# Turning all attention weights by VectorE squares and copies within SBUF, on one core of Trainium2

## The chip, the cores and the metric

One core of a Trainium2 chip runs the kernel. Its engines each work through a queue of their own: TensorE (PE; its weight loads are shown apart as PEld), VectorE (DVE), ScalarE (ACT), GpSimd (POOL), and SyncE (SP), which issues the transfers (DMA). Tiles lie in SBUF (128 partitions) or in PSUM, the accumulators of TensorE. The metric is the device time of one execution in microseconds; before the change it is the median of three runs, 765.46 us (765.05 to 765.88).

## The reference

One encoder layer, for a prompt of 1024 frames and a sample group of 32 frames with a past of 512, in float32, width 1024:

```python
u = rmsnorm(h, g_pre) @ w_in                 # qA kA vA gA qB kB vB gB
# A: 8 heads of 64, a frame sees its 64-frame chunk and the 8 chunks before it
s = einsum('bqhd,bkhd->bhqk', q, k) * ATTN_SCALE + bias_table[:, rel]
oA = einsum('bhqk,bkhd->bqhd', softmax(where(ok, s, NEG_INF)), v)
# B: 8 heads of 64, stick-breaking, causal = (k_pos < q_pos)
z = einsum('bqhd,bkhd->bhqk', q, k) * ATTN_SCALE
log_1m = where(causal, log_sigmoid(-z), 0.0)
after = cumsum(log_1m, axis=3, reverse=True) - log_1m
oB = einsum('bhqk,bkhd->bqhd', where(causal, exp(log_sigmoid(z) + after), 0.0), v)
y = concat(oA * silu(gA), oB * silu(gB)) @ w_out
h = h + rmsnorm(y, g_post)
h = h + sigmoid(h @ w_ple_gate) * (p @ w_ple)
```

The new keys and values are outputs as well.

## The kernel before

**Stages.** The frames are normalised and turned; the projection is made in 32 pieces (8 kinds times 4 pairs of heads, over 3 chunks of 352 frames; PSUM tiles `mm_kB3_2` and the like: kind kB, pair 3, chunk 2); the 16 heads of attention are woven into it, the heads of a kind and pair as soon as their q, k and v are there; the output projection and the gate (`oB`, `gB`, `sum_dro`, `sggA`) end the kernel. Every float32 product is made from a high and a low half (names with h and l, such as `hnh` and `hnl`, `wTh` and `wTl`), in three matmuls.

**A head.** `attention(ab, p, h)` works for kind A or B, pair p, head h; A30 is kind A, pair 3, head 0. It goes over 8 blocks of 128 queries. Block i of B meets i + 1 blocks of keys, block i of A at most 5 (128 to 640 columns). `scores(i)` makes the scores in PSUM tiles of tag S (two pieces, where there are over 512 columns). For A, VectorE adds the bias and takes the minimum (`om`, `stat`), and ScalarE's Exp writes `be`. For B, VectorE adds a mask to the diagonal 128 columns, ScalarE's Sigmoid writes `om`, VectorE's scan multiplies along the row from the right, and GpSimd's subtraction of neighbours writes `be`. `weights_t(i)` turns the weights so that keys lie on partitions, and splits them in the halves `wTh` (a cast on ScalarE) and `wTl` (a subtraction on VectorE). `values(g)` makes the product with v for four blocks of queries (`PV`, g = 0 or 1), first with `wTh`, then with `wTl`; ScalarE and VectorE add the two halves of the result up into `ot` (`otA30_0` is g = 0).

**Two ways to turn.** `ROUND` (line 32) names the blocks that are turned without TensorE: blocks 4 to 7 of A, 4 to 6 of B, one at a time. There VectorE transposes squares of 32 x 32 (STREAM_TRANSPOSE `om<-be`), one transfer writes the result to DRAM in another order (`swapA<-om`), another brings it back (`be<-swapA`), and the halves are made from SBUF. All other blocks are turned by TensorE (`ptw`, up to four 128 x 128 squares in one PSUM tile of tag T), and the halves are made from PSUM. The sample's attention (`sample_attention`: SsA, SsB, QsA, ptks, ptws) uses the same PSUM tags.

**What sets the order.** A `Recorder` collects all operations with what each depends on. `plan()` then sets one order for all engines by a table of costs (`cost()`), `due()` gives due times for 42 further passes, and `settle()` applies some 230 moves by hand (`MOVES`, line 44). `emit()` (line 552 in the profile, whose rows all bear it) issues the operations in that order. Each engine's queue is worked off strictly in order. PSUM has 8 banks: `PS_BUFS = {"mm": 2, "S": 3, "T": 2, "PV": 1}`.

Of the kernel before, what the change touches and what calls it, by code (L numbers as in the profile page):

```python
# [14 lines left out]
P = 128  # L15
# [16 lines left out]
ROUND = {"A": ((4,),(5,),(6,),(7,)), "B": ((4,),(5,),(6,))}  # L32
# [11 lines left out]
MOVES = (  # L44
# [28 lines left out]
)  # L73
PASSES, SPREAD = 42, 400
# [134 lines left out]
class Op:  # L209
    __slots__ = ("eng", "what", "args", "kw", "key", "busy", "late", "ready", "left", "after", "at", "size", "shared", "table")  # L210


LAND = {"PE": 165, "ACT": 0, "DVE": 0, "POOL": 0, "SP": 0, "CTL": 0}
SEM = 60
WAKE = {"PE": 400, "ACT": 100, "DVE": 100, "POOL": 190, "SP": 0}
ISSUE, ISSUE_64, ISSUE_SHORT = 470, 610, 660
DMA_RATE, LANDING, WAKE_DMA = 320.0, 2500, 200
TABLE_NS = 1310
DVE_SET, POOL_SET = 137, 110
# [79 lines left out]
class Recorder:  # L299
# [35 lines left out]
    def node(self, eng, what, args, kw, after):  # L335
        o = Op()
        o.eng, o.what, o.args, o.kw, o.after = eng, what, args, kw, after
        o.key = (self.cls if eng == "PE" else self.low, len(self.ops))
        o.shared, o.table, o.busy, o.late = False, None, 0.0, 0.0
        self.ops.append(o)  # L340
        return o

    def add(self, eng, what, args, kw):
# [22 lines left out]
        o.busy, o.late = self.cost(eng, method, args, kw, writes, reads)  # L366
        o.shared = eng == "POOL"
        o.table = next((a for a in args if a in (AF.Exp, AF.Sigmoid)), None) if eng == "ACT" else None
        if eng == "DVE":
            sbuf = [v for v in reads if isinstance(v, (View, Segments)) and not v.buf.psum and v.free() > 4]  # L370
            o.shared = len(sbuf) > 1 or (method == "tensor_copy" and len(sbuf) == 1 and not writes[0].buf.psum)

    @staticmethod
    def cost(eng, method, args, kw, writes, reads):

# [9 lines left out]
        if eng == "DVE":  # L385
            if method == "tensor_tensor_scan":
                return 150 + 2.1 * n, 85
# [1600 lines left out]
```

## Time and profile before

| | |
|---|---|
| median of three runs | 765.46 us |
| span of the profiled execution | 764.2 us |
| granted clock of TensorE | 1.000 |
| HBM read and written | 107.62 MB and 65.30 MB |
| transfers on SP's queue | 736 |
| VectorE instructions on the weights' way in the order: STREAM_TRANSPOSE `om<-be` / wTl from SBUF / wTl from PSUM | 56 / 56 / 80 |

The profile is of one execution. Each group is written as line, engine, operation, output<-input (partitions x elements), then the count, the busy time in microseconds and the mean of one in nanoseconds, then the idle time of the engine just ahead of these instructions and what ended it. In a timeline a row has its start, its length, the engine and the operation; neighbours of one kind are joined with their count.

### The profile page before, as it was taken

Reading aid. Unit: us, or ns where it says so; the run is one execution under the profiler, and the core shown is the slowest. Engines: PE = TensorE matmul, PEld = TensorE weight load, DVE = VectorE, ACT = ScalarE, POOL = GpSimd, SP = SyncE. Lnnn points to the kernel's source line nnn. Section 1 sums busy time; section 2 is a strip of 40 time slices with the busy share of each in tenths; the row PEclk is TensorE's granted clock in tenths of the full one; section 3 lists DMA queues with packets and bytes.
Section 4 is the critical chain, followed back from the end, with each engine's and each line's share of the span. In section 5 each row is a group of like instructions: output and inputs, shape, how many; then the busy total and the mean of one; then the engine's idle time right before and its main releaser. Section 6 shows DMA issues by size and latency. Waiting matters only on the chain.

```text
span 764.2 us, 13673 instructions
## 1 busy us (share of the span) xinstructions
PE 757.5 (99%) x4422; PEld 702.8 (92%) x4422; DVE 582.2 (76%) x1025; ACT 490.2 (64%) x995; POOL 455.2 (60%) x525
## 2 busy tenths in 40 slices
PE   9999999999999999999999999999999999999997
PEld 7999999999999999999999999999998877888786
DVE  6826789888899888988998798884554588587665
ACT  5736686567685658785668685633447868774551
POOL 5705637874344546566882346786543769898443
PEclk9999999999999999999999999999999999999999
DMA  8519998877976649999678789787688859879854
GB/s 275 175 36 277 294 297 280 236 235 252 247 225 187 181 135 283 275 317 293 173 243 274 173 244 275 222 255 225 192 271 267 275 161 330 278 250 336 277 183 139
DMA packets 184826, 182.25 MB, mean 238 GB/s; under 512 B 42177, under 2 KB 139497, under 8 KB 184754
## 3 DMA queue, kind: packets, MB, share of 16 engines
q1 hardware_dynamic: 184754, 181.37, 78.3%
q8 instruction: 35, 0.57, 0.3%
q14 instruction: 37, 0.30, 0.1%
HBM read 107.62 MB, written 65.30 MB: 226 GB/s over the span
## 4 chain that ended last, share of the span: by engine, by line
PE 99%; DMA 1%; DVE 0%; SPq 0%; issue 0%
PE mm_qA L552 6%; PE mm_kA L552 6%; PE mm_vB L552 6%; PE mm_vA L552 6%; PE mm_gA L552 6%; PE mm_gB L552 6%; PE mm_kB L552 6%; PE mm_qB L552 6%; PE SB L552 5%; PE PVB L552 4%; PE PVA L552 4%; PE SA L552 4%; PE ple L552 3%; PE g1P L552 3%; PE o3P L552 3%; PE o1P L552 3%
## 5 line engine op out<-in xcount | busy, mean ns | idle before, releaser
L552 POOL TENSOR_TENSOR be<-om 128x128 f32<-128x128 f32 (+7 forms) x64 | 77.9, 1224 | 57.1 <-DVE om L552 29.8
L552 DVE TENSOR_TENSOR_SCAN om<-om,SB 128x384 f32<-128x384 f32 (+5 forms) x96 | 94.5, 998 | 7.6 <-ACT om L552 5.0
L552 DVE TENSOR_TENSOR wTl<-be,wTh 128x640 fp32r<-128x640 f32 (+2 forms) x56 | 60.7, 1087 | 5.3 <-ACT wTh L552 5.2
L552 ACT ACTIVATE om<-SB 128x384 f32<-128x384 f32 (+5 forms) x96 | 45.0, 492 | 29.3 <-PE SB L552 12.4
L552 ACT ACTIVATE be<-om,statA 128x640 f32<-128x640 f32 (+3 forms) x64 | 46.4, 730 | 14.6 <-DVE wTl L552 7.3
L552 DVE STREAM_TRANSPOSE om<-be 128x640 f32<-128x640 f32 (+2 forms) x56 | 49.6, 891 | 5.4 <-ACT be L552 3.4
L552 ACT CAST wTh<-be 128x640 fp32r<-128x640 f32 (+2 forms) x56 | 43.1, 776 | 12.3 <-DMA be<-swapA 6.6
L552 ACT CAST wTh<-ptwB 128x512 fp32r<-128x512 f32 (+3 forms) x48 | 22.1, 485 | 20.5 <-PE ptwB L552 15.1
L552 DVE CUSTOM_DVE_ANT_0 om<-SA,biasA 128x320 f32<-128x320 f32 (+3 forms) x64 | 29.7, 483 | 6.9 <-PE SA L552 6.2
L552 POOL TENSOR_TENSOR gB<-gB,gB 128x256 f32<-128x256 f32 x32 | 25.9, 828 | 12.3 <-DMA gB<-in_w_ple_gate_dram 6.2
L552 PE MATMUL SB<-klB,LB 128*128 128x384 f32 (+5 forms) x96 | 33.0, 347 | 0.0
L552 PE MATMUL SB<-kdB,LB 128*128 128x384 f32 (+5 forms) x96 | 32.5, 344 | 0.0
L552 DVE TENSOR_TENSOR wTl<-ptwB,wTh 128x512 fp32r<-128x512 f32 (+3 forms) x48 | 25.3, 541 | 6.6 <-PE PVB L552 3.9
L552 POOL TENSOR_TENSOR oB<-oB,oB 128x256 f32<-128x256 f32 x32 | 26.1, 841 | 6.8 <-DMA oB<-in_w_out_dram 6.7
L552 PE MATMUL SA<-klA,LA 128*128 128x320 f32 (+2 forms) x96 | 29.5, 319 | 0.0
L552 PE MATMUL SA<-kdA,LA 128*128 128x320 f32 (+2 forms) x96 | 29.4, 316 | 0.0
L552 DVE TENSOR_TENSOR SB<-SB,maskb 128x128 f32<-128x128 f32 x64 | 18.3, 291 | 14.3 <-PE SB L552 13.8
L552 POOL TENSOR_TENSOR sggA<-sggA,oggA 128x352 f32<-128x352 f32 x24 | 25.6, 1069 | 5.7 <-DMA o_dr<-otA 2.7
L552 POOL TENSOR_TENSOR klB<-stkB,kdB 64x1024 fp32r<-64x1024 f32 x8 | 19.2, 2396 | 10.7 <-ACT kdB L552 7.3
L552 POOL TENSOR_TENSOR klA<-stkA,kdA 64x1024 fp32r<-64x1024 f32 x8 | 19.5, 2436 | 8.1 <-ACT kdA L552 7.8
L552 POOL TENSOR_TENSOR h<-h,x 128x512 f32<-128x512 f32 (+1 forms) x18 | 23.1, 1295 | 1.5 <-DVE h L552 1.4
L552 POOL TENSOR_TENSOR sggB<-sggB,oggB 128x352 f32<-128x352 f32 x12 | 13.2, 1100 | 14.4 <-DVE sggB L552 14.4
(683 smaller groups left out, 2591.1 us busy)
## 6 DMA issues: line engine op xcount, KB each, us to landing
swapA<-om SPq DMA_DIRECT2D x32, 320.0 KB
be<-swapA SPq DMA_DIRECT2D x32, 320.0 KB
oB<-in_w_out_dram SPq DMA_DIRECT2D x16, 256.0 KB
sum_dro<-oB SPq DMA_DIRECT2D x16, 256.0 KB
gB<-in_w_ple_gate_dram SPq DMA_DIRECT2D x16, 256.0 KB
sum_drg<-gB SPq DMA_DIRECT2D x16, 256.0 KB
x<-in_x_prompt_dram SPq DMA_DIRECT2D x16, 256.0 KB
turned<-hs SPq DMA_DIRECT2D x16, 256.0 KB
```

What stands on the lines that cost most here:

```text
L552: getattr(getattr(tc.nc, o.what[0]), o.what[1])(*args, **kw)
```

## The change

`ROUND` becomes `((0,1,2,3),(4,),(5,),(6,),(7,))` for both kinds. Blocks 0 to 3 of a head are turned together, with 1280 columns; block 7 of B, with 1024, is turned like the others. No weight of the prompt is turned by TensorE (224 transposes go). A round's two transfers through DRAM become four copies within SBUF, each from 32 source partitions to all 128. The operation ahead (Exp of A, the subtraction of B) writes `be` in the order that one transpose of the whole round needs. Neighbouring blocks of a round are split into halves by one cast and one subtraction. The mask of B goes from VectorE, ahead of the sigmoid, to GpSimd, behind it, as a fill with 1.0. PSUM tag S has four buffers and T one. `plan()`, `cost()`, `due()`, `settle()`, `MOVES` and their constants go: `ORDER` holds, for each engine, the numbers of its operations in the order in which they are issued.

```diff
-ROUND = {"A": ((4,),(5,),(6,),(7,)), "B": ((4,),(5,),(6,))}
+ROUND = {"A": ((0, 1, 2, 3), (4,), (5,), (6,), (7,)), "B": ((0, 1, 2, 3), (4,), (5,), (6,), (7,))}
...
-MOVES = (
-    (4286, 4279), (4263, 4256), (2107, 2084), (9133, 9126), (3839, 3830), (1137, 1124), (110, 105), (5252, 5215), (100, 94), (682, 676), (1066, 1059),
...
+ORDER = {
+    "PE": """
+0-23 48-53 24-27 54-61 28-31 62-71 84-85 32-35 72-81 36-39 86 82-83 87-89 40-43 90-95 120-123 144 44-47 145-147 124-132 96-99 133-143 148-149 100-103 150-160
...
-    PS_BUFS = {"mm": 2, "S": 3, "T": 2, "PV": 1}
+    PS_BUFS = {"mm": 2, "S": 4, "T": 1, "PV": 1}
...
+        def first(i):
+            g = together[i]
+            return sum(cost(x) for x in g[:g.index(i)])
+
-        def apart(i, x, out=False):
+        def apart(i):
 
             if i not in together:
-                return x
-            return x.rearrange("p (c k d) -> p k c d" if out else "p (k c d) -> p k c d", c=2, d=2)
+                return rooms(i)[1]
+            g = together[i]
+            n = sum(cost(x) for x in g) * P
+            rooms(i)
+            return whole[g][1][:, 0:n].rearrange("p (c k d) -> p k c d", c=2, d=2)[:, first(i) * 32:(first(i) + cost(i)) * 32]
+
+        def keys(i, x):
+            return x.rearrange("p (k c d) -> p k c d", c=2, d=2) if i in together else x
...
-                dg = s[:, b - a - P:b - a]
-                nc.vector.tensor_tensor(dg, dg, maskb, ALU.add)
                 nc.gpsimd.memset(w0[:, n:n + 1], 1.0)
                 for a, b, s in pieces:
                     nc.scalar.activation(w0[:, a:b], s, AF.Sigmoid, scale=-1.0)
+                nc.gpsimd.affine_select(out=w0[:, n - P:n], in_=w0[:, n - P:n], pattern=[[-1, P]], base=0, channel_multiplier=1, compare_op=ALU.is_gt, fill=1.0)
...
-                nc.gpsimd.tensor_tensor(apart(i, w1[:, 0:n], True), apart(i, w0[:, 1:n + 1]), apart(i, w0[:, 0:n]), ALU.subtract)
+                nc.gpsimd.tensor_tensor(apart(i), keys(i, w0[:, 1:n + 1]), keys(i, w0[:, 0:n]), ALU.subtract)
...
-                for x, _, _ in done_with:
-                    y = slice(first[x], first[x] + cost(x))
-                    nc.vector.transpose(squares[:, :, :, y], w1[:, y.start * P:y.stop * P].rearrange("p (i b k j) -> p i j b k", i=2, k=32, j=2))
-                dr = scratch([4, P, m * 32], f"swap{nm}_{i}")
-                dma(dr.rearrange("g (k c) x -> (g k) (c x)", c=4), w0[:, 0:m * P])
-                dma(w1.rearrange("p (g x) -> p g x", g=4), dr.rearrange("g p x -> p g x"))
-                turned = w1.rearrange("p (g b q) -> p g b q", g=4, q=32)
-                for x, hi, lo in done_with:
-                    src = turned[:, :, first[x]:first[x] + cost(x), :]
-                    hi, lo = (y.rearrange("p (b g q) -> p g b q", g=4, q=32) for y in (hi, lo))
+                nc.vector.transpose(squares, w1[:, 0:m * P].rearrange("p (i b k j) -> p i j b k", i=2, k=32, j=2))
+                for g4 in (0, 2, 1, 3):
+                    dma(w1[:, g4 * m * 32:(g4 + 1) * m * 32], w0[32 * g4:32 * g4 + 32, 0:m * P].rearrange("k (c x) -> k c x", c=4))
+                turned = w1[:, 0:m * P].rearrange("p (g b q) -> p g b q", g=4, q=32)
+                runs = []
+                for x, c in sorted(done_with):
+                    if runs and runs[-1][1] + runs[-1][2] * P == c and runs[-1][0] + runs[-1][2] == first(x):
+                        runs[-1][2] += cost(x)
+                    else:
+                        runs.append([first(x), c, cost(x)])
+                for x, c, k in runs:
+                    src = turned[:, :, x:x + k, :]
+                    hi, lo = (y[:, c:c + k * P].rearrange("p (b g q) -> p g b q", g=4, q=32) for y in wT[g])
                     nc.scalar.copy(hi, src)
                     nc.vector.tensor_tensor(lo, src, f(hi), ALU.subtract)
```

The written order differs from the planned one over the whole of the attention. Two places are shown; in the rows, the line (552 before, 493 of the changed kernel) is followed by the operation, output<-input with their numbers, and the columns.

First place, TensorE before, from the end of PVA30_0 (head A30, blocks 0 to 3) towards the sample's scores SsA1:

```order
L552 MATMUL PVA30_0_5246<-wTl_188,v2A30_4836 128x128
L552 MATMUL ptksA11_5290<-ident_179,be_211 128x128 x4
L552 MATMUL mm_kB3_2_5148<-hnh2_175,wl_kB3_0_4814 128x352
L552 MATMUL SA31_1_0_5306<-kdA31_4990,LA31_4995 128x256
L552 MATMUL SA31_1_0_5306<-klA31_4994,LA31_4995 128x256
L552 MATMUL mm_kB3_2_5148<-hnh2_175,wl_kB3_0_4814 128x352 x2
L552 MATMUL mm_kB3_2_5148<-hnh2_175,wl_kB3_1_4861 128x352 x4
L552 MATMUL mm_kB3_2_5148<-hnl2_178,wh_kB3_0_4878 128x352
```

Behind these rows stand 30 more projection matmuls of kB3 and qB3 ahead of the first SsA1, and more between the SsA1. TensorE at the same place after the change:

```order
L493 MATMUL PVA30_0_5252<-wTl_131,v2A30_4901 128x128
L493 MATMUL mm_qB3_2_5191<-hnl2_122,wh_qB3_1_4980 128x352
L493 MATMUL SA31_2_0_5379<-kdA31_4939,LA31_4941 128x384
L493 MATMUL SA31_2_0_5379<-klA31_4940,LA31_4941 128x384
L493 MATMUL SsA1_0_5317<-Kh0sA1_4741,QsA1_5377 128x272
L493 MATMUL SsA1_272_5329<-Kh0sA1_4741,QsA1_5377 128x272
L493 MATMUL SsA1_0_5317<-Kl0sA1_4754,QsA1_5377 128x272
L493 MATMUL SsA1_272_5329<-Kl0sA1_4754,QsA1_5377 128x272
```

One projection matmul now stands between PVA30_0 and SsA1. Behind the twelve SsA1 follow SA31_4_1 to SA31_6_1, four matmuls of mm_vB3_0 and PVA30_1. VectorE at this place before and after, from the addition otA30_0 on (ISA is the bias and minimum of A's scores; the small rows fill `stat`):

```order
L552 TENSOR_TENSOR otA30_0_5003<-PVA30_0_5246,otA30_0_5003 64x512
L552 ISA om_197,statA31_1_5200<-SA31_1_0_5306,biasA31_5220 128x256
L552 ISA statA31_1_5200 128x1
L552 STREAM_TRANSPOSE om_197<-be_211 128x640
L552 RECIPROCAL sumsA30_4084<-sumsA30_4084 128x8
L552 TENSOR_TENSOR Kl1sA1_5138<-ptksA11_5290,Kh1sA1_5115 128x512
L552 TENSOR_TENSOR wTl_188<-be_211,wTh_527 128x4x5x32
L552 STREAM_TRANSPOSE ktB3_5235<-stkB3_5039 128x1056
```

```order
L493 TENSOR_TENSOR otA30_0_5188<-PVA30_0_5252,otA30_0_5188 64x512
L493 ISA om_138,statA31_0_5267<-SA31_0_0_5273,biasA31_5272 128x128
L493 ISA statA31_0_5267 128x1
L493 ISA om_138,statA31_1_5318<-SA31_1_0_5331,biasA31_5272 128x256
L493 ISA statA31_1_5318 128x1
L493 STREAM_TRANSPOSE om_138<-be_145 128x640
L493 ISA om_138,statA31_2_5330<-SA31_2_0_5379,biasA31_5272 128x384
L493 ISA statA31_2_5330 128x1
L493 STREAM_TRANSPOSE om_138<-be_145 128x640
L493 TENSOR_TENSOR wTl_131<-be_145,wTh_476 128x4x5x32
L493 RECIPROCAL sumsA30_4225<-sumsA30_4225 128x8
L493 TENSOR_TENSOR LB30_5277<-stqB3_5143,LB30_5277 64x1024
```

After the change two transposes of 640 columns stand behind otA30_0. Behind LB30 follow QsA1, a second subtraction of 5 blocks, the two SsA1, SA31_3_0 to SA31_4_1 with a third subtraction, the transpose of 1280 columns, and the fourth subtraction.

Second place, TensorE after the change, from the end of PVB10_0 (head B10) to the sample's scores SsB0:

```order
L493 MATMUL PVB10_0_3079<-wTl_131,v2B10_2685 128x128
L493 MATMUL mm_qA2_2_3249<-hnh2_119,wh_qA2_1_2897 128x352 x4
L493 MATMUL mm_qA2_2_3249<-hnh2_119,wl_qA2_0_2882 128x352 x4
L493 MATMUL mm_qA2_2_3249<-hnh2_119,wl_qA2_1_2898 128x352 x4
L493 MATMUL mm_qA2_2_3249<-hnl2_122,wh_qA2_0_2881 128x352 x2
L493 MATMUL SB11_2_0_3307<-kdB11_2682,LB11_2684 128x384
L493 MATMUL SB11_2_0_3307<-klB11_2683,LB11_2684 128x384
L493 MATMUL mm_qA2_2_3249<-hnl2_122,wh_qA2_0_2881 128x352 x2
L493 MATMUL mm_qA2_2_3249<-hnl2_122,wh_qA2_1_2897 128x352 x4
L493 MATMUL SsB0_0_3182<-Kh0sB0_2991,QsB0_3300 128x272
```

There the twelve SsB0 follow, with PVB10_1 among them. VectorE there, from otB10_0 on, before and after (SCALAR_TENSOR_TENSOR is the scan):

```order
L552 TENSOR_TENSOR otB10_0_3110<-PVB10_0_3184,otB10_0_3110 64x512
L552 TENSOR_TENSOR Kl1sB0_3031<-ptksB01_3160,Kh1sB0_3012 128x512
L552 TENSOR_TENSOR SB11_1_0_3268<-SB11_1_0_3268,maskb_181 128x128
L552 STREAM_TRANSPOSE ktA2_3099<-stkA2_2807 128x544
L552 TENSOR_TENSOR Kl0sB0_2977<-ksS_184,Kh0sB0_2955 128x32
L552 SCALAR_TENSOR_TENSOR om_197<-om_197,SB11_1_0_3268 128x256
```

```order
L493 TENSOR_TENSOR otB10_0_3080<-PVB10_0_3079,otB10_0_3080 64x512
L493 TENSOR_TENSOR wTl_131<-be_145,wTh_476 128x4x5x32
L493 SCALAR_TENSOR_TENSOR om_138<-om_138,SB11_0_0_3128 128x128
L493 TENSOR_TENSOR wTl_131<-be_145,wTh_476 128x4x6x32
L493 SCALAR_TENSOR_TENSOR om_138<-om_138,SB11_1_0_3216 128x256
L493 TENSOR_TENSOR wTl_131<-be_145,wTh_476 128x4x7x32
L493 TENSOR_TENSOR QsB0_3300<-QfsB0_3092,QsB0_3300 128x256
L493 TENSOR_TENSOR LA20_3133<-stqA2_2807,LA20_3133 64x1024
L493 TENSOR_TENSOR wTl_131<-be_145,wTh_476 128x4x8x32
```

All four subtractions of the second half (5 to 8 blocks of keys) now stand behind otB10_0, and behind the last of them the scans of SB11_2_0 and of the sample.

More of the change, by code (lines that the diff above doesn't have):

```diff
@@ L1 @@
-import random
 from contextlib import ExitStack
@@ new lines @@
+3151-3166 3232-3235 3167-3170 3236-3239 3171-3174 3177-3194 3240-3383 3388-4197
+""",
+    "ACT": """
+0 4 2 1 3 5 7-8 6 15-17 9 18 10 19-20 12 11 22 25 13-14 28 21 23 33 24 38 26 34 27 41 30 29 37 31-32 44 39 47 40 42 48 43 45-46 49 35 50 36 53 61 51 62 55 52 60
+63-65 54 67-68 74 56 66 73 80 71 77 70 69 57 79 58 81 76 75 86 78 83 59 72 82 84 88 90 105 89 91 85 92 98 101 93 99 97 96 87 94-95 106 104 107 100 108 111 103
+118 102 109 121 110 112 123 122 125-126 113 119 114 120 128 124 129 127 133 132 136 131 135 115 139 116 142 144 150 138 143 148 141 137 130 134 117 147 140
@@ new lines @@
+758 754 765 764 753 771 770 760 774 768 776-777 775 766 783 779 781 767 784 780 785 761 794 786-787 778 795 798 797 772-773 799 796 788-789 782 803 800 807-808
+805-806 812 811 790-793 815 804 818 809 801-802 820 814 813 810 824 816 822 817 826 819 825 829 821 830 827 833-834 831 823 836 828 835 838 832 837 840 839 842
+841 843-846 848 847 849 851 850 852-856 858 857 859-860
+""",
+    "POOL": """
+0 4 1 48 65 2-3 9-10 5-6 11 7-8 12-13 15-16 14 19 17 21 20 18 22 27-28 23 29 24 30-31 25 32 26 35-41 46-47 63-64 33-34 43 42 49-50 45 44 61 59-60 62 77 154 75
@@ L209 @@
 class Op:
[L210 to L219, printed above, removed]
+    __slots__ = ("eng", "what", "args", "kw", "after")
 class Pool:
@@ L365, in add @@
                 b.uses.append((o, v.box, write))
[L366 to L371, printed above, removed]
@@ L416, in order @@
             place.after.update(x[0] for x in old.uses)
-        users = {id(o): [] for o in self.ops}
-        for o in self.ops:
-            for a in o.after:
-                users[id(a)].append(o)
-        spread = random.Random(22)
-        best, end = self.plan(users)
-        for _ in range(PASSES):
-            self.due(best, users, end)
-            for o in self.ops:
-                if o.eng not in ("CTL", "PE"):
-                    o.key = (o.key[0] + spread.gauss(0, SPREAD), o.key[1])
-            best, end = self.plan(users)
@@ L429, in order @@
-        return self.settle(best)
-    @staticmethod
-    def settle(ops):
-        for i, j in MOVES:
-            x = ops[i]
-            need, engines, ahead, behind = set(x.after), {x.eng}, [], []
-            for o in reversed(ops[j:i]):
-                if o in need or (o.eng in engines and o.eng != x.eng):
-                    assert o.eng != x.eng
-                    ahead.append(o)
-                    need |= o.after
-                    if o.eng != "CTL":
-                        engines.add(o.eng)
-                else:
-                    behind.append(o)
-            ops[j:i + 1] = ahead[::-1] + [x] + behind[::-1]
-        return ops
@@ L449, in due @@
-    def due(self, out, users, end):
-        late, after = {}, {}
-        for o in reversed(out):
-            e = o.eng
-            t = after.get(e, end) if 0 and e != "CTL" else end
-            for u in users[id(o)]:
-                v = late[id(u)]
-                if u.eng == e and e not in ("SP", "CTL"):
-                    v -= 0.0 if e == "PE" else o.late
-                elif u.eng != "CTL":
-                    v -= SEM + WAKE[u.eng] + (WAKE_DMA if e == "SP" and u.eng != "SP" else 0) + o.late * (e != "SP")
-                elif e != "SP":
-                    v -= o.late
-                if e == "SP":
-                    v -= LANDING + o.late
-                t = min(t, v)
-            if e == "PE":
-                right = min(t, after.get(e, end)) - o.busy
-                after[e] = right
-                late[id(o)] = o.at + 1.0 * max(0.0, right - o.at)
-                continue
-            late[id(o)] = t - o.busy if e != "CTL" else t
-            if e != "CTL":
-                after[e] = late[id(o)]
-                o.key = (late[id(o)], o.key[1])
@@ new lines, in order @@
+        mine = {e: [o for o in self.ops if o.eng == e] for e in ORDER}
+        lines = {}
+        for e, text in ORDER.items():
+            runs = [[int(x) for x in run.split("-")] for run in text.split()]
+            lines[e] = [mine[e][i] for r in runs for i in range(r[0], r[-1] + 1)]
+            assert len(lines[e]) == len(set(lines[e])) == len(mine[e])
+        out, done, places = [], set(), [o for o in self.ops if o.eng == "CTL"]
+        at = dict.fromkeys(lines, 0)
+        while len(out) < len(self.ops):
+            n = len(out)
+            for o in [x for x in places if x.after <= done]:
+                out.append(o)
+                done.add(o)
+                places.remove(o)
+            for e, line in lines.items():
+                while at[e] < len(line) and line[at[e]].after <= done:
+                    out.append(line[at[e]])
+                    done.add(line[at[e]])
+                    at[e] += 1
+            assert len(out) > n
@@ L542, in emit @@
+        return out
     def emit(self, tc):
```

226 lines of the change are left out of this document (119 added, 107 removed), and 27 rows, old and new, of the table MOVES.

## The prediction
> **What bounds the kernel now.** I read three views, from coarse to fine: the page's busy times and its chain, then a window table of the attention stage.
>
> ```profile
> span 764.2 us, 13673 instructions
> PE 757.5 (99%) x4422; PEld 702.8 (92%) x4422; DVE 582.2 (76%) x1025; ACT 490.2 (64%) x995; POOL 455.2 (60%) x525
> PE 99%; DMA 1%; DVE 0%; SPq 0%; issue 0%
> 100.00:500.00 400.00, 400.00 (x2546) 388.85 (x2545) 349.23 (x621) 276.24 (x566) 232.40 (x282) 1.00 0.82 240
> ```
>
> The second line is busy time by engine, the third the chain that ended last, and the fourth the stretch from 100 to 500 us: its length, then busy time and count of PE, PEld, VectorE, ScalarE and GpSimd, then the granted clock, the DMA share and GB/s. TensorE is never idle, and its clock is 1.00. So only less TensorE work, or a gap torn into it, can move the time. The last line holds the warning: VectorE is already busy 349.23 of those 400 us (87%).
>
> **Taken from TensorE.** The transposes of the attention weights go: 144 of B and 80 of A.
>
> ```profile
> L552 PE MATMUL ptwB<-ident,be 128*128 128x128 f32 x144 | 21.6, 273 | 0.0
> L552 PE MATMUL ptwA<-ident,be 128*128 128x128 f32 x80 | 13.5, 272 | 0.0
> 409.02 0.93 PE L552 MATMUL ptwA<-ident,be 128*128 128x128 f32 x7
> 409.71 1.05 PE L552 MATMUL mm_kB<-hnl,wh_kB 128*128 128x352 f32 x5
> 70.40 0.49 PE L552 MATMUL ptwA<-ident,be 128*128 128x128 f32 x3
> 70.64 0.40 PE L552 MATMUL SA<-klA,LA 128*128 128x320 f32 x1
> ```
>
> The mean of 272 ns is pipeline depth and not what a transpose occupies. The last four rows (start, length, what) give that: seven transposes from 409.02 to 409.71 are 0.099 us each, three from 70.40 to 70.64 are 0.080 each. 224 of them are 17.9 to 22.1 us. I take 0.087, **-19.4 us**, as more of them stand in short groups like the second.
>
> **Added to VectorE.** 16 transposes of 1280 columns and 8 of 1024 come in, 64 mask additions go, and of the subtractions that make the low half (wTl) 80 from PSUM give way to 56 from SBUF: 16 each of 128, 256 and 896 columns, 8 of 1024.
>
> ```profile
> L552 DVE STREAM_TRANSPOSE om<-be 128x640 f32<-128x640 f32 x40 | 33.0, 834 | 4.3 <-ACT be L552 3.4 <-POOL be L552 0.6
> L552 DVE STREAM_TRANSPOSE vxB<-stvB 128x1024 f32<-128x1024 f32 x4 | 4.9, 1234 | 0.0
> L552 DVE TENSOR_TENSOR wTl<-be,wTh 128x640 fp32r<-128x640 f32 x40 | 40.3, 1012 | 2.6 <-ACT wTh L552 2.4
> L552 DVE TENSOR_TENSOR wTl<-be,wTh 128x896 fp32r<-128x896 f32 x8 | 9.9, 1241 | 1.1 <-ACT wTh L552 1.1
> L552 DVE TENSOR_TENSOR wTl<-ptwB,wTh 128x512 fp32r<-128x512 f32 (+3 forms) x48 | 25.3, 541 | 6.6 <-PE PVB L552 3.9 <-ACT wTh L552 2.5
> L552 DVE TENSOR_TENSOR wTl<-ptwA,wTh 128x128 fp32r<-128x128 f32 (+3 forms) x32 | 15.0, 475 | 2.8 <-PE PVA L552 1.6 <-ACT wTh L552 1.1
> L552 DVE TENSOR_TENSOR SB<-SB,maskb 128x128 f32<-128x128 f32 x64 | 18.3, 291 | 14.3 <-PE SB L552 13.8
> ```
>
> A transpose grows by 400 ns for 384 columns, so 1280 columns are about 1.50 us; the 24 are 16 x 1.50 + 8 x 1.23 = 33.9. The mask gives back 18.3. The subtractions: 229 ns for 256 columns puts 128, 256 and 1024 at 0.55, 0.67 and 1.36, so 16 x (0.55 + 0.67 + 1.24) + 8 x 1.36 = 50.2 against 25.3 + 15.0 = 40.3, +9.9. Together 33.9 - 18.3 + 9.9 = **+25.5 us**. If a small subtraction costs in SBUF what the shorter ones cost in PSUM (0.3 less), the 32 small ones make it +16. I take +20, as 128 and 256 columns have no row in SBUF. Spread over the 485 us or so of attention, 349 becomes some 366 us in a stage that TensorE would cover in 400 - 16 = 384: 95% instead of 87%. On average it still fits. What decides is whether the written order makes the two meet.
>
> **Where they don't meet: two places.** The order (shown in the section on the change) fixes on VectorE what stands between the addition that ends a head's first half (otA30_0, otB10_0) and the last wTl that its second half needs. That addition waits for the first half's last matmul, so TensorE gets only what the order puts behind that.
>
> ```profile
> 413.07 0.80 PE L552 MATMUL PVA<-wTl,v2A 128*128 128x512 f32 x4
> 413.90 0.58 ACT L552 COPY otA<-PVA 64x512 f32<-64x512 f32 x1 [0.60 <-PE PVA L552]
> 414.52 0.68 DVE L552 TENSOR_TENSOR otA<-PVA,otA 64x512 f32<-64x512 f32 x1
> 415.13 0.41 DVE L552 CUSTOM_DVE_ANT_0 om<-SA,biasA 128x256 f32<-128x256 f32 x1
> 416.92 1.46 PE L552 MATMUL mm_qB<-hnh,wh_qB 128*128 128x352 f32 x8
> 418.21 1.46 PE L552 MATMUL mm_qB<-hnh,wl_qB 128*128 128x352 f32 x8
> 420.64 0.41 PE L552 MATMUL SsA<-Kh0sA,QsA 128*128 128x272 f32 x2
> 420.88 0.41 PE L552 MATMUL SsA<-Kl0sA,QsA 128*128 128x272 f32 x2
> L552 DVE CUSTOM_DVE_ANT_0 om<-SA,biasA,statA 128x320 f32<-128x320 f32 x32 | 17.1, 539 | 2.0 <-PE SA L552 1.6
> L552 DVE CUSTOM_DVE_ANT_0 om<-SA,biasA 128x128 f32<-128x128 f32 x8 | 2.2, 278 | 1.9 <-PE SA L552 1.6 <-POOL biasA L552 0.3
> L552 DVE CUSTOM_DVE_ANT_0 om<-SA,biasA 128x512 f32<-128x512 f32 x8 | 5.5, 686 | 1.2 <-PE SA L552 1.2
> L552 DVE TENSOR_TENSOR LB<-stqB,LB 64x1024 fp32r<-64x1024 f32 x8 | 10.8, 1350 | 0.5 <-ACT LB L552 0.2
> L552 DVE TENSOR_TENSOR LA<-stqA,LA 64x1024 fp32r<-64x1024 f32 x8 | 12.7, 1589 | 5.5 <-ACT LA L552 5.3
> L552 DVE TENSOR_TENSOR_SCAN om<-om,SB 128x384 f32<-128x384 f32 x24 | 23.9, 995 | 2.0 <-ACT om L552 1.9
> L552 DVE TENSOR_TENSOR QsB<-QfsB,QsB 128x256 fp32r<-128x256 f32 x2 | 1.2, 579 | 0.0
> L552 DVE CUSTOM_DVE_ANT_0 om<-SsA,biassA 128x272 f32<-128x272 f32 x2 | 0.9, 442 | 3.2 <-PE SsA L552 3.2
> ```
>
> First place, head A30 to A31, with the sample's attention between. TensorE: a projection matmul of 352 columns starts every 0.161 us (418.21 - 416.92 over 8), one of 272 every 0.12. Behind PVA30_0 stand one projection, two scores of 384, twelve SsA, twelve scores of 320, two of 512, then projections and the high half of PVA30_1: by columns 6.4 us to the first wTl of PVA30_1. VectorE in the same stretch: one ot addition 0.61, eight scores together 3.4 (128, 256, 384 and 512 columns on a line from 0.28 to 0.69, four of 320 at 0.5), two transposes of 640 at 0.77, one of 1280 at 1.43, four subtractions at 0.94, LB 1.3, QsA 0.5 (as QsB), two SsA 0.8, small ones 0.25: 13.7 us with 0.07 off each duration, the overlap that the third row and the fourth show (414.52 + 0.68 against 415.13), and 0.65 from the matmul's end to the addition (413.87 to 414.52). 13.7 + 0.65 - 6.4 = **8.0 us** of gap. Before, some seventy projection matmuls stood there, 11 us of cover.
>
> Second place, B10 to B11: VectorE from otB10_0 to the scans of the sample has 10.7 us (four subtractions of 640 to 1024 columns 4.6, five scans of 128 to 384 together 3.3, LA20 1.5, QsB 0.5, ot and the sample's mask 0.8, with the same overlap), and 0.65; TensorE has 6.0 us of projections, SsB0 and PVB10_1. Gap **5.4 us**. With the shortest durations of subtraction and LB or LA in the trace, the two gaps are 7.0 and 4.1.
>
> **Other edits.**
>
> ```profile
> L552 POOL TENSOR_SCALAR_AFFINE_SELECT maskb<-maskb x1: 292/292/292, 1.7 to 1.7; 128x128 f32<-128x128 f32 x1
> L552 SPq DMA_DIRECT2D swapA<-om x32: 319/390/1623, 75.6 to 449.4; - x32
> L552 SPq DMA_DIRECT2D be<-swapA x32: 359/492/2756, 84.3 to 453.2; - x32
> L552 SPq DMA_DIRECT2D kdA<-kdA x8: 482/510/638, 57.3 to 390.6; - x8
> DVE wTl L552 <- ACT wTh L552: 5.2, 9, 1.1
> DVE om L552 <- ACT om L552: 5.0, 7, 1.8
> ```
>
> The mask on GpSimd: 64 x 0.292 = 18.7 us, where 232.40 of 400 are busy; hidden, but each fill stands between a sigmoid and its scan, so it adds a step for VectorE to wait. The permuted subtraction has no row: from no change to twice its 77.9 us, still under GpSimd's free time; I take no change, as the same 128 columns move. ScalarE has 24 casts fewer and stays hidden (276 of 400 busy). One PSUM buffer for sample transposes instead of two, four for scores instead of three: only a few groups use the first, so between -2 and +3, taken as 0. On the queue of SP, 320 copies replace 112 transfers: from 112 x 0.44 = 49 to 320 x 0.50 = 160 us, which moves every other issue behind them later. The trip itself has one hop less, but four issues (2.0 us) stand where two (0.88) stood. Bounds: -10 (earlier arrival, nothing waits) to +18 (1.1 us in the last round of 16 heads). The nearest row is a copy within SBUF, kdA, whose issue alone costs 0.51, so the issue decides; here taken as hidden, and kept as a rival.
>
> Last, the rest of VectorE's waits. In 100 to 500 us it waited 24 us for engines other than TensorE (the two largest are the last two rows above, 10.2 together). With 95% load that slack is no longer free. Between 0 and 24; I take a third, **+8**.
>
> **Sum.** 764.2 - 19.4 + 8.0 + 5.4 + 8 = 766.2 us of span. The median of the runs, 765.46, lies 1.26 above the profiled span, so **767.5 us**: no gain, within a fraction of a per cent. 0.2% is 1.5 us, about what a measurement of this kernel can tell from no change.
>
> **Rivals.** *TensorE stays the bound.* Waits hide, the two gaps take their short values: 764.2 - 19.4 + 7.0 + 4.1 + 1.3 = **757**. For it: TensorE idles nowhere now, and a third of the loss needs no mechanism that I can point to. Against it: the two gaps are forced by the order, and nothing gives them back.
>
> *The copies bind.* The round that turns a head's last block now needs a transpose, four issues and a landing before its PV. Where the order leaves less than about 5 us there, TensorE waits: four issues against two is 1.1 us, 16 heads make 17, and 767.5 + 16 = **783**. It decides from the point at which SP reaches a round's copies after VectorE has turned it. For it: SP's issues grow by 110 us in the attention stage. Against it: SP waits for VectorE (45.5 us for om), so it is mostly ready.
>
> ```profile
> SPq L552 <- DVE om L552: 45.5, 30, 9.8
> ```
>
> That row is SP's own waiting. [...] No row of this profile shows a source of 32 partitions.
>
> *The change doesn't do what it says* is excluded by the counts of the order: no ptw transpose is left.
>
> **How the numbers follow.** Forecast case 47% (763 to 773: the last term between 4 and 13), TensorE bound 33%, copies 20%. The range 753 to 784 reaches into both rivals: 753 is the 757 with its gaps a third shorter (11.1 / 3 = 3.7), 784 the copies case. The forecast case alone splits 3 to 14 to 30 (its middle lies 0.27% above 765.46). Faster 33 + 3 = 36%, same 14%, slower 30 + 20 = 50%.
>
> **What would show it.** The two gaps: TensorE idle before PVA30_1's wTl matmuls and before SsA1 and SsB0, 8 and 5.4 us, put down to VectorE. TensorE's busy time down by 19.4 and its idle time up by over 15. VectorE's stage at 95%. If TensorE's idle time is put down to ScalarE's wTh with copies (be from om) behind it, the second rival is right; if it is under 8 us in all, the first. I would be wrong in the whole if VectorE's shares change price: a subtraction of 1280 columns that runs against GpSimd may cost more than its line.

## The result, and the profile after

The changed kernel takes 821.3 us (median of 4 runs, 819.91 to 822.88) against 765.67 us of the kernel before beside it (4 runs, 765.05 to 766.55): a ratio of 1.0723, 95% interval 1.0700 to 1.0746. It is 7.2% slower. The forecast was 767.5 us, with 784 as the upper end.

The page of the changed kernel (span, busy times, the chain that ended last) and the window from 100 to 500 us, with columns as in the prediction:

```profile
span 818.4 us, 13597 instructions
PE 758.4 (93%) x4198; PEld 685.4 (84%) x4198; DVE 602.8 (74%) x961; ACT 491.5 (60%) x973; POOL 488.2 (60%) x589
PE 45%; DMA 17%; SPq 11%; DVE 11%; ACT 7%; issue 5%; POOL 4%; DVEq 0%; POOLq 0%; ACTq 0%
100.00:500.00 400.00, 361.31 (x2130) 337.27 (x2129) 329.31 (x521) 253.77 (x499) 232.51 (x307) 0.98 0.78 206
```

TensorE was on the chain for 99% before; now for 45%, with transfers and SP's queue together at 28%. TensorE is idle 38.7 of the 400 us, and over the whole span 60.0 us (818.4 - 758.4), where it was 6.7 before. VectorE has not become the bound: it is busy 329 us there (82%), since it waits as well. That alone speaks against the forecast, which had VectorE at 95%.

What TensorE waits for, the four largest rows of its waits (total in us, times, longest):

```profile
PE SA L493 <- DVE statA L493: 8.6, 9, 3.4
PE SsA L493 <- ACT QsA L493: 8.0, 1, 8.0
PE SsB L493 <- ACT QsB L493: 6.5, 2, 3.3
PE PVB L493 <- ACT wTh L493: 3.8, 4, 1.7
```

These rows do not end at a cause, since the engines that they name wait themselves. So the next step is the waits of ScalarE, VectorE and GpSimd, and the issues on SP's queue (duration of one: min, median, max in ns, then first and last start):

```profile
ACT wTh L493 <- DMA be<-om: 45.8, 32, 4.7
DVE om L493 <- DMA be<-om: 19.0, 10, 7.7
POOL om L493 <- DMA be<-om: 27.5, 17, 3.8
L493 SPq DMA_DIRECT2D be<-om x320: 542/602/2028, 75.8 to 594.6; - x160
```

All three wait for the copies from `om` to `be`: ScalarE for the turned weights, VectorE and GpSimd because they may not write the next scores into a piece of the `om` ring that a copy has yet to read. One issue takes SP 0.60 us at the median, so a round's four are 2.4 us and all 320 are 193 us.

### The profile page after: what moved, and what is told of

Its sections match the earlier page's. It is cut to its first block, busy times and chain, and to the rows that moved or that the text cites. A ratio compares the mean times of both kernels' runs of the same rounds, so it can differ in the third digit from the quotient of the medians.

```text
span 818.4 us, 13597 instructions
## 1 busy us (share of the span) xinstructions
PE 758.4 (93%) x4198; PEld 685.4 (84%) x4198; DVE 602.8 (74%) x961; ACT 491.5 (60%) x973; POOL 488.2 (60%) x589
## 2 busy tenths in 40 slices
DMA packets 193275, 177.01 MB, mean 216 GB/s; under 512 B 45505, under 2 KB 155113, under 8 KB 193202
## 4 chain that ended last, share of the span: by engine, by line
PE 45%; DMA 17%; SPq 11%; DVE 11%; ACT 7%; issue 5%; POOL 4%; DVEq 0%; POOLq 0%; ACTq 0%
SPq L493 11%; DMA be<-om 8%; PE mm_gB L493 6%; DVE om L493 5%; DVE wTl L493 3%; PE g1P L493 2%; PE o3P L493 2%; PE o1P L493 2%; PE g2P L493 2%; PE g0P L493 2%; PE o0P L493 2%; PE o2P L493 2%; PE g3P L493 2%; PE ple L493 2%; PE mm_vA L493 2%
## 5 line engine op out<-in xcount | busy, mean ns | idle before, releaser
L493 DVE TENSOR_TENSOR wTl<-be,wTh 128x640 fp32r<-128x640 f32 (+5 forms) x112 | 101.2, 925 | 18.3 <-ACT wTh L493 17.8
L493 ACT CAST wTh<-be 128x640 fp32r<-128x640 f32 (+5 forms) x112 | 74.7, 695 | 48.7 <-DMA be<-om 45.8
L493 DVE STREAM_TRANSPOSE om<-be 128x640 f32<-128x640 f32 (+4 forms) x80 | 83.2, 1044 | 8.9 <-POOL be L493 5.1
L493 POOL TENSOR_SCALAR_AFFINE_SELECT om<-om 128x128 f32<-128x128 f32 x64 | 33.2, 526 | 29.1 <-ACT om L493 24.2
L493 ACT ACTIVATE om<-SB 128x384 f32<-128x384 f32 (+5 forms) x96 | 43.1, 494 | 11.3 <-PE SB L493 7.3
L493 DVE CUSTOM_DVE_ANT_0 om<-SA,biasA 128x320 f32<-128x320 f32 (+4 forms) x64 | 29.2, 481 | 25.2 <-DMA be<-om 19.0
L493 PE MATMUL SA<-kdA,LA 128*128 128x320 f32 (+4 forms) x96 | 31.5, 345 | 9.6 <-DVE statA L493 8.6
L493 PEld LDWEIGHTS SA<-kdA,LA 128*128 128x128 f32 x96 | 18.8, 199 | 13.6 <-DVE statA L493 11.5
L493 PE MATMUL SA<-klA,LA 128*128 128x320 f32 (+4 forms) x96 | 29.6, 331 | 0.5 <-DMA klA<-klA 0.5
L493 POOL TENSOR_TENSOR wl_vB<-wr_vB,wh_vB 128x512 fp32r<-128x512 f32 x8 | 10.9, 1367 | 28.9 <-ACT wh_vB L493 13.4
L493 POOL TENSOR_TENSOR klB<-stkB,kdB 64x1024 fp32r<-64x1024 f32 x8 | 19.5, 2432 | 13.6 <-ACT kdB L493 13.4
L493 PE MATMUL PVB<-wTh,v2B 128*128 128x512 f32 (+1 forms) x96 | 22.2, 351 | 4.6 <-ACT wTh L493 3.8
L493 PEld LDWEIGHTS SB<-kdB,LB 128*128 128x128 f32 x96 | 18.1, 189 | 8.3 <-DVE om L493 4.2
```

What stands on the lines that cost most here:

```text
L493: getattr(getattr(tc.nc, o.what[0]), o.what[1])(*args, **kw)
```

## The experiments

Most of these kernels leave work out or put it elsewhere, so that one part of the cost can be seen by itself. The theories: **A**, the way of the copies (their issues on SP's queue, their landing, their bytes) is what the engines wait for. **B**, the written order is too tight on VectorE and ScalarE, whatever the copies cost (the forecast's own reason). Each kernel had one timed run; beside them the kernel before took 765.7 to 767.7 us, so differences under 3 us say nothing.

**One copy of four.** In `weights_t`, only the copy with g4 = 0 is issued; three quarters of the weights are not turned. Operations marked `skip` are not issued.

```diff
+                if o.skip:
+                    continue
...
                 for g4 in (0, 2, 1, 3):
                     dma(w1[:, g4 * m * 32:(g4 + 1) * m * 32], w0[32 * g4:32 * g4 + 32, 0:m * P].rearrange("k (c x) -> k c x", c=4))
+                    rec.ops[-1].skip = g4 != 0
```

> The changed kernel with one of a round's four copies issued (the first quarter of be; the other three quarters of the weights are left out, so the output differs). 80 issues on SP's queue in place of 320, a quarter of the bytes, the order of everything else as written. Theory A (the route: issues and landing of the copies are what the engines wait for): 770 to 785 us, ScalarE's wait of wTh for be from om falls from 45.8 us to under 15. Theory B (the written order itself is too tight on VectorE and ScalarE, whatever the copies cost): over 800 us. By theory A the wait of 8.0 us ahead of SsA1 shrinks too, by B it stays.

Measured: 770.88 us, 50.4 less than the changed kernel with the same order on every engine. The page's second line, ScalarE's wait for the copies, and TensorE's at the first place:

```profile
PE 746.0 (97%) x4198; PEld 681.0 (89%) x4198; DVE 601.0 (78%) x961; ACT 489.8 (64%) x973; POOL 492.9 (64%) x589
ACT wTh L496 <- DMA be<-om: 2.1, 2, 1.7
PE SsA L496 <- ACT QsA L496: 5.0, 1, 5.0
```

VectorE's load is the same to within 2 us (601.0 and 602.8), and 50 us are gone: theory A. But 5.0 of the 8.0 us ahead of SsA1 stay, so a part of that place does not hang on the other three copies.

**Small copies.** All four issued, each of a quarter of its columns; three quarters of the weights are not turned.

```diff
-dma(w1[:, g4 * m * 32:(g4 + 1) * m * 32], w0[32 * g4:32 * g4 + 32, 0:m * P].rearrange("k (c x) -> k c x", c=4))
+dma(w1[:, g4 * m * 32:g4 * m * 32 + m * 8], w0[32 * g4:32 * g4 + 32, 0:m * P].rearrange("k (c x) -> k c x", c=4)[:, :, 0:m * 8])
```

> The changed kernel with all four copies of a round issued, each of a quarter of its columns (three quarters of the turned weights are left out, so the output differs). Same bytes as with one copy, but 320 issues. If the issues on SP's queue are the price: 805 to 820 us, as the changed kernel. If the bytes and the ports are: 770 to 785 us, as with one copy. Theory B: over 800 us in both.

Measured: 802.84 us. With the bytes of one copy but all the issues, 32.0 of the 50.4 us are back; the remaining three quarters of the bytes bring 18.5. It fits neither expectation alone: issues and bytes both count, the issues more; of ports no run shows anything. The 32.0 us are not the queue's time alone, though: a round waits for four landings again, and the transfers have as many packets (the pieces in which they move) as in the changed kernel, 193275, where one copy has 158710.

**One copy and dummies.** The other three issues of a round go from a constant (`ident`) to DRAM, and nobody waits for them; three quarters of the weights are not turned.

```diff
+                    if g4 == 0:
                         dma(w1[:, g4 * m * 32:(g4 + 1) * m * 32], w0[32 * g4:32 * g4 + 32, 0:m * P].rearrange("k (c x) -> k c x", c=4))
+                    else:
+                        dma(scratch([P, 32], f"dummy{nm}_{i}_{g4}").rearrange("(k c) x -> k c x", c=4), ident[32 * g4:32 * g4 + 32, :].rearrange("k (c x) -> k c x", c=4))
```

> As one_copy (770.9 us; three quarters of the weights are left out), but the three missing copies of a round are replaced by copies of 16 KB from a constant to DRAM, for whose landing nothing waits. SP's queue has 320 issues again. If the time in SP's queue is what the issues cost (everything behind them starts later): 795 to 805 us, as small_copies (802.8). If it is that a round is complete only with its fourth copy: within 6 us of 770.9.

Measured: 790.28 us, between the two. 19.4 us come with the issues, though nobody waits for their landing: the time on SP's queue, and 3.9 MB more of writing to DRAM (240 issues of 16 KB), which this run does not separate. The other 12.6 up to small_copies appear when a round also has to wait for its fourth copy; small_copies has 23043 packets more as well, and their share was not measured. ScalarE's wait for the copies follows, 2.1, then 13.0 here, then 27.7 with the small copies:

```profile
ACT wTh L493 <- DMA be<-om: 13.0, 10, 4.1
```

**Same bytes, all partitions.** The four copies take pieces of the same size from all 128 partitions; the weights land in a wrong layout, so the turning is left out.

```diff
-dma(w1[:, g4 * m * 32:(g4 + 1) * m * 32], w0[32 * g4:32 * g4 + 32, 0:m * P].rearrange("k (c x) -> k c x", c=4))
+dma(w1[:, g4 * m * 32:(g4 + 1) * m * 32], w0[:, g4 * m * 32:(g4 + 1) * m * 32])
```

> The changed kernel with the four copies of a round taking the same bytes in as many pieces straight from all 128 partitions, in place of 32 partitions each (the weights land in a wrong layout, so the turning is left out in effect). If reading from 32 partitions is what makes the 18.5 us between small_copies and the changed kernel: 803 to 810 us. If it is the bytes alone: 816 to 824 us.

Measured: 810.22 us. 11.1 of the 18.5 us that go with the bytes are gone when the copies read from all 128 partitions; 7.4 stay. This lies on the edge of the first expectation, and the split is good to about 3 us.

**Two queues.** Two of a round's four copies are issued by ScalarE; they stand in its order by the times at which they and ScalarE's operations started in the changed kernel's profile (those lines are left out here).

```diff
+                    if g4 in (1, 3):
+                        o = rec.ops[-1]
+                        o.moved, o.what = True, ("scalar", "dma_start")
```

> The changed kernel with the last two copies of each round issued by ScalarE's queue, at the place in ScalarE's order that the profile of the changed kernel has at that time; SP keeps 160 of the 320. If SP's queue is the bottleneck: 780 to 800 us, less what 160 issues cost ScalarE. If the bytes and the landing are, or if the issues cost any engine the same: 810 us or more.

Measured: 811.24 us, 10 less than the changed kernel. The issues by queue:

```profile
L502 ACTq DMA_DIRECT2D be<-om x160: 550/572/2225, 76.5 to 585.6; - x160
L502 SPq DMA_DIRECT2D be<-om x160: 542/597/1958, 78.0 to 584.5; - x160
```

The issue costs ScalarE the same 0.57 us. Relief for SP is real, but ScalarE pays 160 x 0.57 = 91 us of its own time, which stands ahead of its casts. Expected was 780 to 800, or 810 and more: it is the second.

**Outputs first.** On SP's queue, each transfer of a finished `ot` to DRAM is put where its `ot` was ready, ahead of the copies.

```diff
+            added = rec.ops[-1]
             dma(o_dr[sidx(ab, p)][r, 4 * g * P:4 * (g + 1) * P], ot[r])
+            rec.ops[-1].ot = added
...
+        when = {id(o): t for t, o in zip(DVE_AT, lines["DVE"])}
+        both = [(min(t, when[id(o.ot)] + 72) if o.ot else t, 0 if o.ot else 1, k, o) for k, (t, o) in enumerate(zip(SP_AT, lines["SP"]))]
+        lines["SP"] = [x[3] for x in sorted(both, key=lambda x: x[:3])]
```

> The changed kernel with one thing moved on SP's queue: each of the 32 transfers of a finished head half (o_dr from ot) stands where its ot was ready in the profile of the changed kernel, ahead of the copies that stood before it. If the wait of SsA1 and SsB0 is VectorE's order, as the prediction had it: 8.0 and 3.3 us stay, and the time stays within 3 us of 821.3. If it is the ot buffer that waits for its transfer behind the copies: the wait at SsA1 falls to 5 us or less, and the time to 805 to 815 us.

Measured: 828.19 us, 7 more. The place itself, first in the timeline of the changed kernel, then of this one (start, length, what, and in brackets the idle time and what ended it):

```profile
460.50 0.74 PE L493 MATMUL PVA<-wTl,v2A 128*128 128x512 f32 x4
461.90 0.68 DVE L493 TENSOR_TENSOR otA<-PVA,otA 64x512 f32<-64x512 f32 x1
465.85 0.55 SPq L493 DMA_DIRECT2D o_dr<-otA  x1
469.32 0.40 ACT L493 CAST QsA<-QfsA 128x256 fp32r<-128x256 f32 x1 [1.66 <-DMA o_dr<-otA]
469.77 0.82 PE L493 MATMUL SsA<-Kh0sA,QsA 128*128 128x272 f32 x2 [7.97 <-ACT QsA L493]
469.80 0.42 DVE L493 TENSOR_TENSOR QsA<-QfsA,QsA 128x256 fp32r<-128x256 f32 x1
...
470.85 0.66 PE L493 MATMUL SsA<-Kh0sA,QsA 128*128 128x272 f32 x2
471.30 0.65 PE L493 MATMUL SsA<-Kh1sA,QsA 128*128 128x272 f32 x2
```

```profile
471.32 0.65 DVE L501 TENSOR_TENSOR otA<-PVA,otA 64x512 f32<-64x512 f32 x1
471.99 0.46 SPq L501 DMA_DIRECT2D o_dr<-otA  x1
475.89 0.41 ACT L501 CAST QsA<-QfsA 128x256 fp32r<-128x256 f32 x1 [0.32 <-DMA o_dr<-otA]
476.35 0.82 PE L501 MATMUL SsA<-Kh0sA,QsA 128*128 128x272 f32 x2 [5.38 <-ACT QsA L501]
```

QsA lies in a buffer that it shares with `ot` (tag "ot", two buffers). So its cast waits until the finished `ot` has landed in DRAM. In the changed kernel that transfer was issued 3.3 us after VectorE had finished (461.90 + 0.68 to 465.85). SP issues without a pause in between: `klB`, an output of keys, a transfer of `gB`, and one copy. Moved up, it goes at once, and the wait is 5.4 us. At SsB0 it fell from 3.24 to 1.76. So the place comes near the second expectation (5 us or less), and the total does not (805 to 815): the copies that were passed are late instead. GpSimd's wait for them ahead of `om` grows from 27.5 to 39.4 us, and TensorE's for ScalarE's `wTh` ahead of PVB from 3.8 to 8.2. **The time in SP's queue does not get less by sorting it.**

**The mask back.** VectorE adds the mask in PSUM ahead of the sigmoid, as before, and the fill on GpSimd is skipped. In VectorE's order the addition stands by time, 0.3 us ahead of the start that its sigmoid had in the changed kernel's profile.

```diff
+                dg = s[:, b - a - P:b - a]
+                nc.vector.tensor_tensor(dg, dg, maskb, ALU.add)
+                extra = rec.ops[-1]
...
+                extra.extra = rec.ops[-1]
                 nc.gpsimd.affine_select(out=w0[:, n - P:n], in_=w0[:, n - P:n], pattern=[[-1, P]], base=0, channel_multiplier=1, compare_op=ALU.is_gt, fill=1.0)
+                rec.ops[-1].skip = True
```

> The changed kernel with the mask added in PSUM by VectorE ahead of the sigmoid, as before, and the fill on GpSimd left away; all else, the order too, as written (the addition stands where its sigmoid stood in the profile). If the step between sigmoid and scan costs as in plan_before_mask (+15.7): 800 to 808 us. If VectorE's load is what counts (+18 us of additions): 822 to 835 us.

Measured: 828.61 us, 7.3 more, as the second expectation had it. In the written order, the mask on GpSimd is worth a little, though less than VectorE's 18 us; it is no part of the loss there.

**The planner instead of the written order.** Seven kernels have the planner of before and no moves by hand, so that the order adapts to each edit. First the kernel before, then the changed kernel's work under that planner:

```diff
-MOVES = (
-    (4286, 4279), (4263, 4256), (2107, 2084), (9133, 9126), (3839, 3830), (1137, 1124), (110, 105), (5252, 5215), (100, 94), (682, 676), (1066, 1059),
...
+MOVES = ()
```

> The kernel before without the moves by hand (MOVES empty), so that its planner alone sets the order: the base for the next kernel. 768 to 785 us by every theory.

> The changed kernel's work (rounds, copies, mask, PSUM buffers) with the planner of before, without moves, in place of the written order. Theory B (the written order is what costs): no slower than the planned kernel before, 750 to 780 us. Theory A (the route costs in any order): 20 us or more above it, 790 to 820 us.

Measured: 770.65 and 841.37 us, the second above both ranges. The change costs 70.7 us under the planner, and 55.6 with the two orders by hand. So the loss does not belong to the written order, which is better than the planned one; whether a third order could hide the copies is not shown. Next, the parts of the change one at a time, on the planned kernel before, and the changed kernel's work with two hops through DRAM in place of four copies:

```diff
-                dma(dr.rearrange("g (k c) x -> (g k) (c x)", c=4), w0[:, 0:m * P])
-                dma(w1.rearrange("p (g x) -> p g x", g=4), dr.rearrange("g p x -> p g x"))
+                for g4 in (0, 2, 1, 3):
+                    dma(w1[:, g4 * m * 32:(g4 + 1) * m * 32], w0[32 * g4:32 * g4 + 32, 0:m * P].rearrange("k (c x) -> k c x", c=4))
```

> The planned kernel before (770.7 us) with the four copies in place of the two hops, and nothing else of the change: 224 issues for 112, on 56 rounds. If the issues are the price: 785 to 805 us (112 more of them, against 208 in the change). If the new rounds are: within 5 us of 770.7.

> As plan_after (841.4 us), but each round goes by two transfers through DRAM, as in the kernel before, in place of the four copies: 160 issues in place of 320. If the four issues a round are the price: 780 to 805 us. If what costs is that 80 rounds instead of 56 take this long a way at all: 825 us or more.

> The planned kernel before with the changed rounds (blocks 0 to 3 together, block 7 of B), still by two hops through DRAM: no weight is turned by TensorE. If the issues are the price (48 more of them than before): 770 to 785 us. If the rounds are: 800 us or more.

> The planned kernel before (770.7 us) with one more round: block 7 of B by two hops through DRAM in place of TensorE's transposes (8 rounds more, 64 transposes fewer). If each new round costs alike, a third of the 118 us of plan_before_rounds: about 800 us or more. If the joint round of blocks 0 to 3 is what costs there: 765 to 785 us.

> The planned kernel before with the mask as a fill on GpSimd behind the sigmoid, and nothing else of the change: within 5 us of 770.7 us if the mask plays no part in the loss; over 780 us if the step between sigmoid and scan is part of it.

| planned kernel | us | against plan_before |
|---|---|---|
| plan_before | 770.65 | |
| only the mask on GpSimd | 786.32 | +15.7 |
| only block 7 of B by hops | 795.05 | +24.4 |
| only the four copies, on 56 rounds | 800.54 | +29.9 |
| only the rounds, by hops | 889.14 | +118.5 |
| all of the change | 841.37 | +70.7 |
| all of it, but hops for copies | 864.04 | +93.4 |

Of the five kernels last announced, four came in the higher of their two ranges; block 7 alone, 795.05 us, lies between its two (765 to 785, and about 800 or more). In plan_before_rounds blocks 0 to 2 of the last head are not turned, since that head runs its blocks backwards; one head of 16 bears little of the time. The table refutes a simple form of theory A, that four issues cost more than two: that is so on the old 56 rounds (+29.9), but when all weights take this way, hops are 22.7 us worse than copies. What costs most is that 80 rounds instead of 56 take a way through the transfer queue at all, with blocks that TensorE used to turn on the spot. Block 7 of B alone, 8 rounds, is 24.4 us for 64 transposes fewer. The parts do not add up to the whole; that they draw on the same queue and the same rings is only argued. How much of the 118.5 is the ring `om` (3568 columns, of which a joint round holds 1280) was not tried, and the changed PSUM buffers were not tried alone.

## Why the prediction was wrong, step by step

- **TensorE loses 19.4 us of work.** The transposes went, but its busy time did not fall (757.5 to 758.4): the rest of its work took 20.3 us longer. Behind some of its waits the granted clock is halved; the windows from 450 to 500 us, of before and of the changed kernel:

```profile
450.00:500.00 50.00, 50.00 (x317) 48.51 (x317) 41.12 (x62) 32.21 (x69) 35.36 (x38) 1.00 0.85 246
450.00:500.00 50.00, 38.71 (x221) 34.88 (x220) 36.96 (x85) 34.57 (x72) 18.31 (x27) 0.90 0.77 197
```

  The granted clock is 0.90 there, around the 7.97 us wait. The SsA rows show it: behind the wait, pairs start 0.45 us apart (470.85 and 471.30), before it was 0.24 (420.64 and 420.88). Over the whole span the clock stood at half for 32 us, and TensorE was busy in 24 of them, so 12 us of work at full speed were lost (an estimate: these pairs take about twice as long at half the clock). Most of the other 8 fits the stops themselves, as an estimate: at each of its 47 waits the end of the last matmul is no longer covered by the next (0.33 us long for 352 columns, 0.161 from start to start), 47 x 0.17 = 8. In this trace the half clock came in pieces of 3.41 us (four), 6.83 and 10.24 us, and one of 1.5 at the end. In the 3.41 us ahead of a piece TensorE had been busy for 0.00 to 1.50 us: for 0.97 in 83.09 to 86.50 us, for 1.50 in 229.86 to 233.27. Behind 513.20 to 516.61, with 1.60 us busy, the clock stayed at 1.00. The forecast priced gaps at their length and left this out.
- **VectorE gains 20 us.** Right in sum: 582.2 to 602.8, partly by luck. The new rows came about as forecast, and the rows that were there before became shorter:

```profile
L493 DVE STREAM_TRANSPOSE om<-be 128x1280 f32<-128x1280 f32 x16 | 23.9, 1495 | 0.3 <-ACT be L493 0.2
L493 DVE STREAM_TRANSPOSE om<-be 128x1024 f32<-128x1024 f32 x8 | 9.9, 1236 | 2.1 <-POOL be L493 2.1
L493 DVE TENSOR_TENSOR wTl<-be,wTh 128x640 fp32r<-128x640 f32 (+5 forms) x112 | 101.2, 925 | 18.3 <-ACT wTh L493 17.8
L493 DVE TENSOR_TENSOR wTl<-be,wTh 128x640 fp32r<-128x640 f32 x40 | 36.8, 929 | 6.0 <-ACT wTh L493 5.9
L493 DVE TENSOR_TENSOR wTl<-be,wTh 128x896 fp32r<-128x896 f32 x24 | 30.8, 1284 | 9.6 <-ACT wTh L493 9.3
L493 DVE TENSOR_TENSOR wTl<-be,wTh 128x1024 fp32r<-128x1024 f32 x8 | 11.3, 1409 | 0.0
L493 DVE TENSOR_TENSOR wTl<-be,wTh 128x256 fp32r<-128x256 f32 x16 | 10.3, 641 | 1.0 <-ACT wTh L493 1.0
L493 DVE TENSOR_TENSOR wTl<-be,wTh 128x128 fp32r<-128x128 f32 x16 | 6.2, 388 | 0.3 <-ACT wTh L493 0.2
```

  The transposes are 33.8 us (forecast 33.9). The new subtractions are 16 each of 128, 256 and 896 columns and 8 of 1024: 6.2 + 10.3 + 16 x 1.284 + 11.3 = 48.3 us (forecast 50.2). The 56 of before fell from 60.7 to about 55.0 (640 columns from 1012 to 929 ns each), for a reason that stays open. So all subtractions together are 101.2 us, against 60.7 + 25.3 + 15.0 = 101.0 before: +0.2 and not +9.9. The other 5 of the 20.6 us were not followed up.
- **The two places.** The waits stand where they were forecast, 8.0 us ahead of SsA1 and 3.2 ahead of SsB0 (forecast 8.0 and 5.4); 3.3 more stand ahead of SsB1, which the forecast did not have. The cover that the order took away was the right half of that step. The engine that ended the wait was another: VectorE's rows were added up to 13.7 us, but SsA1 waited for ScalarE's QsA, that for the landing of `ot`, that for SP. With one copy of four the transfer of `ot` goes at once (426.19), QsA still starts only at 429.70, and 5.0 us of wait are left. VectorE is not cleared by this: in the changed kernel it came to its own part of QsA at 469.80, TensorE started at 469.77. A size that fits is no proof of the mechanism.
- **The mask hidden on GpSimd.** Under-priced in the mean, by one row at 1.7 us, when little else ran:

```profile
L493 POOL TENSOR_SCALAR_AFFINE_SELECT om<-om 128x128 f32<-128x128 f32 x64 | 33.2, 526 | 29.1 <-ACT om L493 24.2 <-DMA be<-om 4.3 <-ACT stkA L493 0.2
L493 POOL TENSOR_SCALAR_AFFINE_SELECT om<-om x64: 288/298/1286, 118.1 to 585.1; 128x128 f32<-128x128 f32 x64
```

  The median, 298 ns, is near the forecast's 292; some fills take up to 1286, so the mean is 526. In the written order the move still gains 7.3 us, under the planner it loses 15.7.
- **The copies "taken as hidden": the step that failed.** The sum has them at nothing; they cost 50.4 of the 55.6 us. The forecast counted the issues (0.50 us each, 160 us in all; in fact 0.60 and 193) and noted that they move every other issue behind them, but priced that at nothing, because SP seemed mostly ready. It did not ask who stands behind 2.4 us of issues on an in-order queue. The transfers of `ot` show it: in the changed kernel's trace they are issued 3.0 us after their `ot` is ready on the mean of 32, before 0.5, and with one copy of four 1.1 (start of the issue less the end of the addition, from the three traces).
- **The rival with the copies** had the right cause, a part of the right place and a third of the price: it charged 1.1 us in the last round of each head, ahead of its PV, 17 us. Ahead of PV, TensorE waits 10.0 us for the halves of the weights, 3.8 in the row shown with the result and these:

```profile
PE PVA L493 <- DVE wTl L493: 3.4, 3, 2.0
PE PVA L493 <- ACT wTh L493: 2.8, 6, 1.1
```

  Its larger waits are elsewhere: for the scores (8.6), behind a VectorE that waits 19.0 us for the copies, and for QsA and QsB (8.0 and 6.5), behind `ot`. Of the 50.4 us, 19.4 come with the issues, 12.6 with waiting for a round's fourth copy, and 18.5 with the bytes. When the copies read from all 128 partitions in place of 32, the time falls by 11.1 us (821.30 to 810.22): a part of the copies' price, and not the main part. Why the number of partitions counts is not shown.
- **The rest.** With one copy of four the span is 769.1 us, and the forecast's sum was 766.2. TensorE is idle 23.1 us there, 16.4 more than before, where the sum added 8.0 + 5.4 + 8 = 21.4; its work is 746.0, not 757.5 - 19.4 = 738.1. So without the copies the forecast would have been near, partly by luck: the two places have 7.0 us (5.4 at SsA1, 1.6 at SsB0) of their 13.4, and the price of the stops and of the clock was missing. No run tests the +8 for the rest of VectorE's waits by itself.

## What to carry to other kernels

Work that left the bound engine for a transfer paid here at the queue that issues it (19.4 us came with the issues), and again where a round waited for its last piece to land (12.6): count the issues, multiply by the issue time of the nearest row, and list what stands behind each group, buffers that wait to be freed too. A latency that is hidden for some blocks need not be hidden for all: under the planner, hops for 80 rounds in place of 56 cost 118.5 us. And price a gap on TensorE with the clock that it costs, here 12 us for some 54 us of waiting.

## What the runs showed of the hardware

With two queues an issue took ScalarE's queue as long as SP's (0.572 and 0.597 us at the median, 160 each), so the second queue moved the price and did not remove it: 10 of 55.6 us were gained. Under the planner, two hops through DRAM beat four copies within SBUF by 29.9 us on 56 rounds and lost 22.7 on 80; why the better of the two ways changes stays open.
